# A one-core Hymba encoder layer: the PSUM banks of the keys' projection and of the first scores, and the planning weight of the last two residual chains

## The chip, the cores and the metric

The kernel runs on one core of a Trainium2 chip, as one program. The metric is the device time of one execution in microseconds (us). A few runs give a median; one more execution was recorded by the hardware profiler, and every row below comes from that one. PE is the matrix engine (TensorE), DVE the vector engine, ACT the scalar engine, POOL the GpSimd engine, and SP the queue that issues the DMA transfers. PSUM, into which PE writes its results, has eight banks of 128 x 512 float32 numbers.

## What is computed

```
mod = silu(c) @ w_ada + b_ada            # six vectors: sh1, sc1, gt1, sh2, sc2, gt2
h   = rmsnorm(x, g_pre_mix) * (1 + sc1) + sh1
proj = h @ w_in                          # q, k, v (512 columns each), then the Hyena group's 1536
q = rope(q); k = rope(k)
attn = dilated_window_attention(q, k, v) # 8 heads of 64
hy   = hyena_mixer(...)                  # long convolutions
mixed = concat(rmsnorm(attn, g_attn_out), rmsnorm(hy, g_hyena_out))
x = x + gt1 * rmsnorm(mixed @ w_out, g_post_mix)
h = rmsnorm(x, g_pre_mlp) * (1 + sc2) + sh2
x = x + gt2 * rmsnorm(square(relu(h @ w_mlp1)) @ w_mlp2, g_post_mlp)
```

One sequence of 512 tokens, width 1024, hidden width 4096, all float32.

## The kernel before

Every product is made from three matmuls: each operand is split into a high part and the rest (whi and wlo of a weight, hh and hl of the activations), and high times high, high times rest and rest times high are summed in one bank (`mm3`, line 605). A weight block of 128 x 512 is loaded by one DMA into a tile `raw`; ACT makes whi, and DVE or POOL makes wlo = raw - whi (`wload`, line 617).

The program is not issued in the order in which it is written. Every operation is recorded, and `Plan.order()` (line 290) then sets the order of each engine's instructions by simulating them with estimated durations. Where several operations are ready it takes the one with the largest priority: the length of the chain that hangs on it, plus a bias, plus a weight `urgent` that the code sets by `plan.local`. Operations with a weight of 600 or more may also be taken if they can start up to 0.5 us after the earliest ready one, those of 1000 or more up to 1.4 us, all others 0.02 us (line 379). An engine issues its instructions strictly in that order, so one that waits holds up everything behind it.

PSUM's eight banks are divided by tags: four of tag pj, two of ps, two of pi. A tile gets a bank of its tag when the previous tile in that bank has been read for the last time. `PS4(n, ..)` (line 593) gives four banks: the four pj for even n, and ps, ps, pi, pi for odd n.

The parts that the rows below speak of:

- The queries (banks pj552 to pj555), keys (pj598 to pj601) and values (pj644 to pj647) are projected one after the other by `proj_tok`, each into the four pj banks. `rotary` (line 1141) reads the queries' and keys' banks on DVE: for each token tile one product ra over 512 columns, two rb of 256, and a sum ra + rb on DVE or POOL.
- Beside them run the Hyena group's inverse transforms, whose results (inv487, inv522, inv523) stand in pi banks until DVE has read them into y512, y545 and y548.
- Also beside them run the late column sums of w_ada (`ada_acc`, line 831): eight blocks `raw` one after another, each added to `acc` by one DVE instruction, with three buffers (tag ra) for accumulator and blocks together; PE then makes a column of `acc` in a pj bank (pa, line 874). acc589 is the sum over raw590 to raw597, acc635 that over raw636 to raw643.
- Attention goes over four pairs of heads. For each pair the queries and keys are turned (pqk704 and pqk707 for the first pair, in ps banks); then for each of four query blocks the scores of two heads are made (s741 and s742 first), masked on DVE, put through exp on ACT, turned (ptr745, ..) and multiplied with the values (pav735, ..). Output projection of the Hyena group (pw) fills PE between them (`out_bank`, line 1216).
- After attention, for each token tile tt, `residual(tt)` (line 1315) is a chain on DVE and ACT: y times gate G, a norm factor ry, the new residual xr, a second norm factor r2, and dg, a diagonal matrix of r2. tt 0 has dg1009, tt 1 dg1016, tt 2 dg1031 and tt 3 dg1038. `to_h2` (line 1326) multiplies xr with dg on PE into ph banks: ph1017 to ph1023 for tiles 0 and 1, ph1039 to ph1045 for tiles 2 and 3. The first block of the MLP (pm) runs over the first 256 tokens and then over the second 256.

Of the kernel before, what the change touches and what calls it, by code (L numbers as in the profile page):

```python
# [554 lines left out]
def tile_hymba_layer(ctx, tc, t, out):  # L555
    nc = tc.nc
    plan = Plan(nc)
# [23 lines left out]
    def S(tag, s="u", dt=F32):  # L581
        return plan.tile(HOME.get(tag, "up"), tag, NB[tag], [P, 512], dt, s)
# [7 lines left out]
    def PS(s="ps", tag="ps"):  # L590
        return plan.tile("pp", tag, 4 if tag == "pj" else 2, [P, 512], F32, s)

    def PS4(n, s):

        return [PS(s, tg) for tg in (("pj",) * 4, ("ps", "ps", "pi", "pi"))[n % 2]]

    def T1(s="t", tag="t1"):
        return plan.tile("tiny", tag, 16, [P, 8], F32, s)
# [6 lines left out]
    def mm3(ps, lh, ll, rh, rl, start, stop):  # L605
        pe.matmul(ps, lh, rh, start=start, stop=False)
        pe.matmul(ps, lh, rl, start=False, stop=False)
        pe.matmul(ps, ll, rh, start=False, stop=stop)
# [8 lines left out]
    def wload(src):  # L617
        raw = S("raw", "raw")
        pre_loads.append(sp.dma_start(raw, src))
        hi, lo = wpair()  # L620
        act.copy(hi, raw)
        lo_of(vp, lo, raw, hi)
        return hi, lo
# [58 lines left out]
    ps = PS("pf", "pi")  # L682
# [4 lines left out]
    ps = PS("pf", "pi")  # L687
# [207 lines left out]
    def step(gen, n=1):  # L895
        for _ in range(n):
            next(gen, None)
# [38 lines left out]
    for d in range(8):  # L936
        ps = PS("px", "pj")
# [9 lines left out]
    for c in range(4):  # L947
        plan.bias = 2900.0 - 100.0 * c
        s = slice(2 * c, 2 * c + 2)
# [47 lines left out]
                mm3(banks[i], wh[:, s], wl[:, s], hT[k][0], hT[k][1], k == 0, k == 7)  # L997
        return banks

    def proj_tok(c0):  # L1000

        banks = [PS("pj", "pj") for _ in range(4)]
        for k in range(8):
            wh, wl = wload(w_in[k * P:(k + 1) * P, c0:c0 + 512])
            for i in range(4):
                s = slice(i * P, (i + 1) * P)
                mm3(banks[i], hT[k][0][:, s], hT[k][1][:, s], wh, wl, k == 0, k == 7)
        return banks
# [132 lines left out]
    def rotary(banks):  # L1141
        res = []
        for tt in range(4):
            a, b = S("qk", "ra"), S("cv", "rb")
            ps4 = banks[tt].rearrange("p (h d) -> p h d", h=NH)
            c_ = rope[:, tt, 0][:, None, :].to_broadcast([P, NH, 64])
            dve.tensor_tensor(out=a.rearrange("p (h d) -> p h d", h=NH), in0=ps4, in1=c_, op=ALU.mult)
            psw = banks[tt].rearrange("p (h s d) -> p h s d", h=NH, s=2)
            bw = b.rearrange("p (h s d) -> p h s d", h=NH, s=2)
            for s_ in range(2):  # L1150
                sn = rope[:, tt, 1, s_ * 32:s_ * 32 + 32][:, None, :].to_broadcast([P, NH, 32])
                dve.tensor_tensor(out=bw[:, :, s_, :], in0=psw[:, :, 1 - s_, :], in1=sn, op=ALU.mult)
            vp.tensor_tensor(out=a, in0=a, in1=b, op=ALU.add)
            res.append(a)
        return res

    qr = rotary(proj_tok(0))
    step(late, 2)
    kr = rotary(proj_tok(512))
    step(late, 2)  # L1160
    vb = proj_tok(1024)
    step(late, 2)
    vh = {}
# [48 lines left out]
    def load_out(g, hf):  # L1212
        row0 = W if g == 0 else 0
        return [wload(w_out[row0 + k * P:row0 + (k + 1) * P, hf * 512:hf * 512 + 512]) for k in range(4)]

    def out_bank(g, tt, hf, m_, ws, tag):

        s = slice(tt * P, (tt + 1) * P)
        bank = PS("pw", tag)
        for k in range(4):  # L1220
            mm3(bank, m_[k][0][:, s], m_[k][1][:, s], ws[k][0], ws[k][1], k == 0, k == 3)
        evac(g, tt, hf, bank)
# [10 lines left out]
    def heads(hp2):  # L1233


        tr = []
        for src, scl in ((qr, -0.125), (kr, 1.0)):
            ps = PS("pqk")
            pe.turn(ps, [src[tt][:, hp2 * P:(hp2 + 1) * P] for tt in range(4)], ident)
            hi, lo = R("cv", "qh"), R("cv", "ql")  # L1240
            act.activation(hi, ps, AF.Copy, scale=scl)
            dve.scalar_tensor_tensor(out=lo, in0=ps, scalar=scl, in1=f(hi), op0=ALU.mult, op1=ALU.subtract)
            tr.append((hi, lo))
        return tr

    qk = [heads(0)]
    for hp2 in range(4):
        (qh, ql), (kh, kl) = qk[hp2]
        a = S("vx", "att")
        att.append(a)  # L1250
        if hp2 == 1:
            step(late, 1)
        if hp2 == 0:
            wg0 = [load_out(0, hf) for hf in range(2)]
        rows = slice(0, 64), slice(64, 128)
        po = [PS("pav", "pi") for _ in range(2)]
        for qb in range(4):
            qs = slice(qb * P, (qb + 1) * P)
            o = slice((qb % 2) * P, (qb % 2 + 1) * P)
            if qb % 2 == 0:  # L1260
                pts = [(plan.tile("att", "pt", NPT, [P, 4, 256], F32R, "pth"),
                        plan.tile("att", "pt", NPT, [P, 4, 256], F32R, "ptl")) for _ in range(2)]

            pss = [PS("s", "pj") for _ in range(2)]
            pe.pair(pss, [[(x[r, qs], y[r, :]) for x, y in ((qh, kh), (qh, kl), (ql, kh))] for r in rows])
            for hh in range(2):
                h, ps = hp2 * 2 + hh, pss[hh]
                pth, ptl = pts[hh]
                sc = S("cv", "sc")
                st = T1("st", "st")  # L1270
                dve.tensor_tensor_reduce(out=sc, in0=ps, in1=mask[:, 384 - qb * P:896 - qb * P], scale=1.0,
                                         scalar=3e38, op0=ALU.add, op1=ALU.min, accum_out=st[:, 0:1])
                last_exp = [act.activation(sc, sc, AF.Exp, bias=st[:, 0:1], scale=-1.0, accum_out=st[:, 2:3])]
                dve.reciprocal(st[:, 3:4], st[:, 2:3])
                if qb == 3 or h < 3 and qb == 1:
                    act.activation(sc, sc, AF.Copy, scale=st[:, 3:4])
                else:
                    pool.tensor_tensor(out=sc, in0=sc, in1=st[:, 3:4].to_broadcast([P, 512]), op=ALU.mult)
                pt = PS("ptr")
                pe.turn(pt, [sc[:, kt * P:(kt + 1) * P] for kt in range(4)], ident)  # L1280
                p3 = pt.rearrange("p (k q) -> p k q", k=4)
                act.copy(pth[:, :, o], p3)
                dve.tensor_tensor(out=ptl[:, :, o], in0=p3, in1=f(pth[:, :, o]), op=ALU.subtract)
                if qb % 2:
                    o2 = slice((qb - 1) * P, (qb + 1) * P)
                    for kt in range(4):
                        vv = vh[kt, h // 4][:, (h % 4) * P:(h % 4 + 1) * P]
                        pe.matmul(po[hh][:, o2], vv, pth[:, kt], start=kt == 0, stop=False)
                        pe.matmul(po[hh][:, o2], vv, ptl[:, kt], start=False, stop=kt == 3)
            if qb == 1 and hp2 < 3:  # L1290
                qk.append(heads(hp2 + 1))

            for u in FILL.get((hp2, qb), ()):
                out_bank(0, u % 4, u // 4, mh, wg0[u // 4], "pj")
        for hh in range(2):
            r = rows[hh]
            act.copy(a[r, :], po[hh][64:128, :])
            dve.tensor_tensor(out=a[r, :], in0=po[hh][0:64, :], in1=a[r, :], op=ALU.add)
# [50 lines left out]
    for tt in range(4):  # L1349
        plan.bias = 200.0 * (4 - tt)  # L1350
        for hf in range(2):
            out_bank(1, tt, hf, ma, wo[hf], "pj" if tt < 2 else ("ps", "pi")[hf])
        plan.local = 700.0 * (tt < 2)
        dgs.append(residual(tt))
        plan.local = 0.0
        if tt % 2:
            plan.bias = 400.0
            plan.local = 700.0 if tt == 1 else 0.0
            to_h2(tt // 2, dgs[-2:])
            plan.local = 0.0  # L1360
# [15 lines left out]
    for half in range(2):  # L1376
        hid = []
        for cc in range(4):
            c0 = half * 2048 + cc * 512
            banks = PS4(cc + 1, "pm")  # L1380
            ws = [wload(w_1[k * P:(k + 1) * P, c0:c0 + 512]) for k in range(8)]
            for th in range(2) if half == 0 and cc == 0 else (None,):
                ts = slice(0, 512) if th is None else slice(th * 256, th * 256 + 256)
                for k in range(8):
                    for i in range(4):
                        s = slice(i * P, (i + 1) * P)
# [10 lines left out]
        for hf in range(2):  # L1397
            cs = slice(hf * 512, hf * 512 + 512)
            banks = PS4(hf + 1, "pf")
            nk = 8 if (half, hf) == (1, 1) else 16  # L1400
            for k in range(nk):
                r0 = half * 2048 + k * P
                wh, wl = wload(w_2[r0:r0 + P, cs])
                for tt in range(4):
                    s = slice(tt * P, (tt + 1) * P)
# [3 lines left out]
            for tt in range(4):  # L1409
                s = slice(tt * P, (tt + 1) * P)  # L1410
# [65 lines left out]
```

## Time and profile before

| | |
|---|---|
| median of 3 runs | 756.44 us (755.32 to 757.17) |
| the profiled execution | 760.61 us; span from first to last instruction 758.8 us |
| mean granted clock of PE, as a share of full speed | 0.986 |
| PE busy | 726.2 us, 96% of the span |
| DVE, ACT, POOL busy | 462.1, 325.1 and 80.9 us |

The granted clock has two levels here, 1.00 (2.4 GHz) and 0.50 (1.2 GHz). A number in brackets at the end of a timeline's row is the idle time of the engine just before it, and the arrow names what ended that time. Durations overlap: a matmul's row begins before the one ahead of it has ended, so rates are read from the starts. A wait for several semaphores is put down to the one that came last.

### The profile page before, as it was taken

Reading aid. Unit: us, or ns where it says so; the run is one execution under the profiler, and the core shown is the slowest. Engines: PE = TensorE matmul, PEld = TensorE weight load, DVE = VectorE, ACT = ScalarE, POOL = GpSimd, SP = SyncE. Lnnn points to the kernel's source line nnn. Section 1 sums busy time; section 2 is a strip of 40 time slices with the busy share of each in tenths; the row PEclk is TensorE's granted clock in tenths of the full one; section 3 lists DMA queues with packets and bytes.
Section 4 is the critical chain, followed back from the end, with each engine's and each line's share of the span. In section 5 each row is a group of like instructions: output and inputs, shape, how many; then the busy total and the mean of one; then the engine's idle time right before and its main releaser. Section 6 shows DMA issues by size and latency. Waiting matters only on the chain.

```text
span 758.8 us, 10203 instructions
## 1 busy us (share of the span) xinstructions
PE 726.2 (96%) x3648; PEld 587.7 (77%) x3648; DVE 462.1 (61%) x886; ACT 325.1 (43%) x631; POOL 80.9 (11%) x80
## 2 busy tenths in 40 slices
PE   5999999999999798999979999999999999999995
PEld 2667878988887676878879888888888888888874
DVE  5597974989686688997786844223222554232256
ACT  5545542234224267898575443213322353232132
POOL 0110400113030012343211000000000000000000
PEclk9999999999999899999989999999999999999998
DMA  9995244423615264261022533222223242123212
GB/s 291 359 391 183 84 153 152 126 98 120 209 34 153 73 217 155 84 192 59 29 93 79 187 106 118 84 84 70 97 81 100 84 152 98 56 75 111 98 50 111
DMA packets 55602, 96.68 MB, mean 127 GB/s; under 512 B 5853, under 2 KB 14301, under 8 KB 55296
## 3 DMA queue, kind: packets, MB, share of 16 engines
q1 hardware_dynamic: 54400, 91.58, 36.7%
q0 software_dynamic: 1008, 4.40, 1.6%
q8 instruction: 28, 0.46, 0.3%
q14 instruction: 22, 0.18, 0.1%
q10 hardware_dynamic: 144, 0.06, 0.0%
HBM read 91.56 MB, written 4.46 MB: 127 GB/s over the span
## 4 chain that ended last, share of the span: by engine, by line
PE 84%; DVE 6%; DMA 5%; ACT 3%; issue 1%; SPq 1%; POOL 0%; DVEq 0%; ACTq 0%; POOLq 0%
PE pm L513 24%; PE pf L513 21%; PE pj L513 17%; PE pw L513 4%; PE pH L513 3%; PE inv L513 3%; DMA raw<-in_w_ada_dram 2%; PE pe L513 2%; DMA raw<-in_w_in_dram 2%; PE pav L513 2%; PE ptr L461 1%; PE po L513 1%; PE s L473 1%; PE ph L513 1%; PE pa L513 1%
## 5 line engine op out<-in xcount | busy, mean ns | idle before, releaser
L513 DVE TENSOR_TENSOR wlo<-raw,whi 128x512 fp32r<-128x512 f32 x177 | 121.1, 696 | 164.7 <-ACT whi L513 94.7
L513 ACT CAST whi<-raw 128x512 fp32r<-128x512 f32 x192 | 116.8, 620 | 192.2 <-PE pf L513 92.0
L513 PE MATMUL pm<-h2l,whi 128*128 128x512 f32 (+1 forms) x288 | 88.3, 370 | 0.3 <-POOL h2l L513 0.3
L513 PE MATMUL pm<-h2h,whi 128*128 128x512 f32 (+1 forms) x288 | 88.2, 371 | 0.2 <-ACT h2h L513 0.2
L513 PE MATMUL pm<-h2h,wlo 128*128 128x512 f32 (+1 forms) x288 | 87.8, 370 | 0.0
L513 PE MATMUL pf<-whi,gl 128*128 128x512 f32 x256 | 85.5, 390 | 0.0
L513 PE MATMUL pf<-wlo,gh 128*128 128x512 f32 x256 | 84.7, 390 | 0.0
L513 PE MATMUL pf<-whi,gh 128*128 128x512 f32 x256 | 84.3, 392 | 0.1
L513 PEld LDWEIGHTS pm<-h2h,whi 128*128 128x128 f32 x288 | 51.7, 188 | 11.0 <-ACT h2h L513 1.0
L513 PEld LDWEIGHTS pm<-h2l,whi 128*128 128x128 f32 x288 | 51.9, 188 | 10.5 <-POOL h2l L513 0.5
L513 PEld LDWEIGHTS pm<-h2h,wlo 128*128 128x128 f32 x288 | 51.7, 188 | 10.3 <-DVE wlo L513 0.5
L513 PEld LDWEIGHTS pf<-whi,gh 128*128 128x128 f32 x256 | 47.8, 188 | 11.6 <-ACT whi L513 0.8
L513 PEld LDWEIGHTS pf<-whi,gl 128*128 128x128 f32 x256 | 48.1, 188 | 10.3
L513 PEld LDWEIGHTS pf<-wlo,gh 128*128 128x128 f32 x256 | 47.6, 188 | 10.8
L513 DVE SCALAR_TENSOR_TENSOR acc<-raw,vec,acc 128x512 f32<-128x512 f32 x56 | 42.7, 763 | 17.3 <-DMA raw<-in_w_ada_dram 17.0
L513 DVE TENSOR_TENSOR r<-r 128x512 f32<-128x512 f32 x32 | 21.7, 687 | 43.2 <-ACT r L513 43.2
L513 ACT ACTIVATE r<-pm 128x512 f32<-128x512 f32 x32 | 18.6, 596 | 53.3 <-PE pm L513 53.3
L513 PE MATMUL pj<-hh,whi 128*128 128x512 f32 x96 | 35.2, 397 | 0.8 <-ACT hh L513 0.8
L513 PE MATMUL pj<-hl,whi 128*128 128x512 f32 x96 | 36.0, 401 | 0.0
L513 POOL TENSOR_TENSOR wlo<-raw,whi 128x512 fp32r<-128x512 f32 x15 | 20.7, 1393 | 142.7 <-PE pj L513 37.8
L513 PE MATMUL pj<-whi,hh 128*128 128x512 f32 x96 | 35.6, 410 | 0.0
L513 PE MATMUL pj<-hh,wlo 128*128 128x512 f32 x96 | 35.4, 397 | 0.0
(245 smaller groups left out, 1360.6 us busy)
## 6 DMA issues: line engine op xcount, KB each, us to landing
raw<-in_w_mlp_dram SPq DMA_DIRECT2D x128, 256.0 KB, 2.8
raw<-in_w_ada_dram SPq DMA_DIRECT2D x96, 256.0 KB, 3.2
raw<-in_w_in_dram SPq DMA_DIRECT2D x48, 256.0 KB, 3.3
raw<-in_w_out_dram SPq DMA_DIRECT2D x16, 256.0 KB, 3.0
H<-hd SPq DMA_DIRECT2D x9, 256.0 KB, 4.9
x<-in_x_dram SPq DMA_DIRECT2D x8, 256.0 KB, 4.7
hd<-H SPq DMA_DIRECT2D x8, 256.0 KB, 2.0
xr<-in_x_dram SPq DMA_DIRECT2D x8, 256.0 KB, 5.1
```

Of the source, the lines that this page charges most:

```text
L461: plan.nc.tensor.transpose(out.ap()[:, i * P:(i + 1) * P], v.ap(), ident.ap())
L473: plan.nc.tensor.matmul(out.ap(), ts[i][0].ap(), ts[i][1].ap(), start=i == 0, stop=i == n - 1)
L513: getattr(e, meth)(*[real(a) for a in args], **{k: real(a) for k, a in kw.items()})
```

## The change

The keys' projection no longer goes into the four pj banks but into ps, ps, pi, pi. The first scores of the first pair of heads go into pi banks (query block 0) and ps banks (query block 1) instead of pj. The residual chains of token tiles 2 and 3 get the weight 650 in place of none.

```diff
-    def proj_tok(c0):
-
-        banks = [PS("pj", "pj") for _ in range(4)]
+    def proj_tok(c0, n=0):
+
+        banks = PS4(n, "pj")
...
     qr = rotary(proj_tok(0))
     step(late, 2)
-    kr = rotary(proj_tok(512))
+    kr = rotary(proj_tok(512, 1))
     step(late, 2)
     vb = proj_tok(1024)
...
-            pss = [PS("s", "pj") for _ in range(2)]
+
+            pss = [PS("s", "pj" if hp2 or qb > 1 else ("pi", "ps")[qb]) for _ in range(2)]
...
-        plan.local = 700.0 * (tt < 2)
+        plan.local = 700.0 * (tt < 2) + 650.0 * (tt > 1)
         dgs.append(residual(tt))
```

PE, ACT and SP issue the same instructions as before, and on balance two of DVE's go to POOL. What changes is the order. In the rows below the number behind the underscore differs between the kernels and means nothing; the name ahead of it is the same tile in both.

**PE, the end of the keys' projection (pj599 to pj601) and the start of the values' (pj644, pj645).** Before:

```order
L513 MATMUL pj601_2475<-wlo625_2527,hh146_725 128x512
L513 MATMUL inv523_2424<-ib211_403,yl543_2394 128x258
L513 MATMUL pj601_2475<-whi624_2519,hl147_735 128x512
L513 MATMUL pa634_2631<-ones2_79,acc589_2192 128x1 x2
L513 MATMUL pj644_2636<-whi649_2533,hh87_336 128x512
L513 MATMUL pj645_2638<-whi649_2533,hh87_336 128x512
L513 MATMUL pj644_2636<-wlo650_2542,hh87_336 128x512
```

With the change:

```order
L513 MATMUL pj601_2493<-whi624_2530,hh146_725 128x512
L513 MATMUL pj644_2619<-whi649_2547,hh87_336 128x512
L513 MATMUL pj601_2493<-wlo625_2544,hh146_725 128x512
L513 MATMUL pj644_2619<-wlo650_2557,hh87_336 128x512
L513 MATMUL pj601_2493<-whi624_2530,hl147_735 128x512
L513 MATMUL pj644_2619<-whi649_2547,hl88_348 128x512
L513 MATMUL pj645_2630<-whi649_2547,hh87_336 128x512
```

The column sum pa634, which waited for a pj bank, no longer stands between the two, and the values' matmuls are mixed with the keys' last ones. 22 values' matmuls then follow the keys' last one before the first transposes pqk704, and 6 more before pqk707; before, pqk704 stood ahead of 57 of the keys' 96 matmuls. Farther on, s741 stands ahead of 60 of the values' 96 matmuls and ptr745 ahead of 7; before, s741 came directly behind the last of them.

**DVE, the reads of the inverse transforms.** Before:

```order
L513 SCALAR_TENSOR_TENSOR acc589_2192<-raw592_2252,vec7_71,acc589_2192 128x512
L513 SCALAR_TENSOR_TENSOR acc589_2192<-raw593_2409,vec7_71,acc589_2192 128x512
L513 TENSOR_TENSOR y545_2457<-inv522_2293,q544_2450 128x255 x2
L513 COPY y545_2457<-inv522_2293 128x2
L513 TENSOR_TENSOR sc2214_2469<-pa588_2342,vec7_71 128x4
L513 TENSOR_TENSOR hyo546_2472<-y545_2457,hy464_1901 128x512
```

With the change:

```order
L513 SCALAR_TENSOR_TENSOR acc589_2192<-raw593_2388,vec7_71,acc589_2192 128x512
L513 SCALAR_TENSOR_TENSOR acc589_2192<-raw594_2394,vec7_71,acc589_2192 128x512
L513 TENSOR_TENSOR y545_2449<-inv522_2293,q544_2435 128x255 x2
L513 COPY y545_2449<-inv522_2293 128x2
L513 TENSOR_TENSOR hyo546_2467<-y545_2449,hy464_1901 128x512
L513 SCALAR_TENSOR_TENSOR acc589_2192<-raw595_2442,vec7_71,acc589_2192 128x512
L513 TENSOR_TENSOR y548_2481<-inv523_2407,q547_2474 128x255 x2
L513 COPY y548_2481<-inv523_2407 128x2
```

y548, the read of inv523, stood inside the keys' rotary (some 30 instructions later) and now stands well ahead of it; but the steps of acc589 for the blocks raw594 and raw595 moved ahead of y545 and y548.

**DVE, from the second tile's xr957 to its dg1016.** Before:

```order
L513 SCALAR_TENSOR_TENSOR xr957_3630<-y778_3097,ry1013_4121,xr957_3630 128x512
L513 SCALAR_TENSOR_TENSOR xr958_3637<-y885_3644,ry1013_4121,xr958_3637 128x512
L513 SCALAR_TENSOR_TENSOR y832_3504<-pw1032_3980,gr954_4009,y832_3504 128x512
L513 TENSOR_TENSOR r21015_4153<-s21014_4140 128x1
L513 TENSOR_TENSOR wlo1076_4155<-raw1074_3953,whi1075_4112 128x512
L513 SCALAR_TENSOR_TENSOR y932_4099<-pw1033_4094,gr954_4009,y932_4099 128x512
L513 RECIPROCAL r21015_4153<-r21015_4153 128x1
L513 TENSOR_SCALAR dg1016_4169<-ident1_81,r21015_4153 128x128
```

With the change:

```order
L513 SCALAR_TENSOR_TENSOR xr957_3595<-y778_3110,ry1013_4108,xr957_3595 128x512
L513 SCALAR_TENSOR_TENSOR xr958_3602<-y885_3669,ry1013_4108,xr958_3602 128x512
L513 TENSOR_TENSOR wlo1070_4130<-raw1068_3891,whi1069_4103 128x512
L513 TENSOR_TENSOR wlo1073_4136<-raw1071_3936,whi1072_3973 128x512
L513 TENSOR_TENSOR r21015_4145<-s21014_4127 128x1
L513 TENSOR_TENSOR wlo1076_4147<-raw1074_3948,whi1075_4120 128x512
L513 RECIPROCAL r21015_4145<-r21015_4145 128x1
L513 TENSOR_SCALAR dg1016_4157<-ident1_81,r21015_4145 128x128
```

The reads of banks pw1032 and pw1033 (y832, y932) moved behind dg1016, and two wlo, which POOL made before, came in. POOL, which made four wlo between dg1009 and dg1016 or just ahead (wlo1067, wlo1073, wlo1070, wlo1079), has two of them left, and ACT makes the cast for the second, wlo1079, later than before. Farther on, the chains of tiles 2 and 3 end together: dg1031 and dg1038 are two instructions apart, where eight lay between them.

## Rows read from the trace of the kernel before

**Rows 1.** The page's part 1: each engine's busy us, share of the span and instructions.
```profile
PE 726.2 (96%) x3648; PEld 587.7 (77%) x3648; DVE 462.1 (61%) x886; ACT 325.1 (43%) x631; POOL 80.9 (11%) x80
```

**Rows 2.** Waits of PE: us in total, times, longest.
```profile
PE pa L513 <- DVE rb L513: 5.8, 1, 5.8
PE ph L513 <- DVE dg L513: 4.1, 1, 4.1
```

**Rows 3.** Busy time, PEclk and DMA in five stretches.
```profile
251.40:257.00 5.60, 5.60 (x16) 4.47 (x17) 4.90 (x12) 1.24 (x2) 0.40 (x1) 0.58 0.17 47
293.60:297.00 3.40, 3.40 (x18) 3.29 (x17) 2.47 (x5) 2.80 (x6) 0.00 (x0) 0.50 0.53 153
297.00:365.00 68.00, 67.75 (x441) 54.51 (x439) 58.31 (x137) 56.73 (x118) 22.19 (x19) 1.00 0.32 101
382.40:389.10 6.70, 4.74 (x22) 4.74 (x23) 5.38 (x14) 4.29 (x12) 1.33 (x1) 0.50 0.29 101
410.00:744.00 334.00, 333.90 (x1480) 272.06 (x1479) 130.41 (x204) 110.84 (x196) 0.00 (x0) 1.00 0.29 97
```

**Rows 4.** Timeline of PE: start, us, instruction [idle before <-releaser].
```profile
250.59 0.99 PE L513 MATMUL pa<-ones,acc 128*128 128x1 f32 x4 [5.80 <-DVE rb L513]
251.44 1.20 PE L513 MATMUL pj<-whi,hh 128*128 128x512 f32 x2
...
255.00 1.05 PE L513 MATMUL pj<-wlo,hh 128*128 128x512 f32 x2
...
256.41 0.62 PE L513 MATMUL pj<-whi,hh 128*128 128x512 f32 x2
256.87 0.64 PE L513 MATMUL pj<-wlo,hh 128*128 128x512 f32 x2
```

**Rows 5.** Timeline of DVE, 222 to 254 us.
```profile
226.64 0.75 DVE L513 SCALAR_TENSOR_TENSOR acc<-raw,vec,acc 128x512 f32<-128x512 f32 x1 [2.69 <-DMA raw<-in_w_ada_dram]
...
244.62 1.77 DVE L513 TENSOR_TENSOR wlo<-raw,whi 128x512 fp32r<-128x512 f32 x1
246.32 0.41 DVE L513 TENSOR_TENSOR rb<-pj,rope 128x256 f32<-128x256 f32 x1
...
251.69 1.88 DVE L513 TENSOR_TENSOR ra<-ra,rb 128x512 f32<-128x512 f32 x3
```

**Rows 6.** Timeline of PE where attention starts.
```profile
279.66 0.80 PE L513 MATMUL pa<-ones,acc 128*128 128x1 f32 x6 [0.66 <-DVE acc L513]
...
291.76 0.66 PE L461 MATMUL ptr<-ident,sc 128*128 128x128 f32 x4 [1.26 <-DVE ptl L513]
293.09 0.39 PE L513 MATMUL pav<-pth,vh 128*128 128x256 f32 x1 [0.68 <-ACT pth L513]
```

**Rows 7.** Timeline of DVE before and at the second dg.
```profile
375.39 1.79 DVE L513 TENSOR_TENSOR y<-y,G 128x512 f32<-128x512 f32 x1
377.11 1.23 DVE L513 TENSOR_TENSOR ry<-sy 128x1 f32<-128x1 f32 x1
378.26 0.68 DVE L513 TENSOR_TENSOR y<-y,G 128x512 f32<-128x512 f32 x1
...
379.05 2.44 DVE L513 SCALAR_TENSOR_TENSOR xr<-y,ry,xr 128x512 f32<-128x512 f32 x2
...
383.86 0.44 DVE L513 TENSOR_SCALAR dg<-ident,r 128x128 f32<-128x128 f32 x1
```

**Rows 8.** Timeline of POOL in the same stretch.
```profile
374.09 4.23 POOL L513 TENSOR_TENSOR wlo<-raw,whi 128x512 fp32r<-128x512 f32 x3 [24.92 <-ACT r L513]
379.26 1.68 POOL L513 TENSOR_TENSOR wlo<-raw,whi 128x512 fp32r<-128x512 f32 x1 [0.94 <-ACT whi L513]
```

**Rows 9.** Timeline of PE around the first half of the MLP's first block.
```profile
384.36 5.23 PE L513 MATMUL ph<-dg,xr 128*128 128x128 f32 x24 [4.06 <-DVE dg L513]
...
401.71 2.92 PE L513 MATMUL ph<-dg,xr 128*128 128x128 f32 x24
...
406.46 0.51 PE L513 MATMUL pm<-h2l,whi 128*128 128x256 f32 x2 [0.31 <-POOL h2l L513]
```

## The prediction

> **What bounds the kernel now.** I read the page's first part first: PE is busy for 96% of the span [rows 1], so a change can win only what PE loses, and no other engine's busy time matters by itself. The list of PE's waits comes next. Two are long, 5.8 us for the keys' rotary and 4.1 us for a dg [rows 2]. Then I asked which stretches have a clock below full speed or PE not filling the time. Attention from 297 us (67.75 of 68.00 us) and the MLP (333.90 of 334.00) have neither [rows 3]: what is won ahead of them should reach the end undiminished. Three places do have such losses, and the change touches all three.
>
> Place 1, the end of the keys' projection. PE stands for 5.80 us until rb instructions have emptied a pj bank, and after it runs at clock 0.50 until about 256 us: five pairs of matmuls, from 251.44 to 255.00, take 1.05 to 1.20 us where a pair takes 0.62 or 0.64 afterwards [rows 3, 4]. With the part of a sixth that is about 5 x 0.43 = 2.2 us more. DVE shows why the rotary is late: the wlo ahead of it took 1.77 us, until 246.39, and the rotary then lasts from 246.32 to 253.57 [rows 5].
>
> Place 2, the start of attention. PE waits 0.66, 1.26 and 0.68 us, and the clock is 0.50 from 293.60 to 297.00, which costs half of 3.40, 1.70 us [rows 3, 6]. Together 4.3 us.
>
> Place 3, the residual. PE waits 4.06 us for dg1016, after which 24 ph matmuls take 5.23 us at clock 0.50 where the same 24 later take 2.92 [rows 3, 9]: 2.2 to 2.3 us more. Smaller waits come to 0.15 + 0.31 us at 405.65 and 406.46; the row with the second is shown [rows 9]. DVE is slow there in three instructions: y times G 1.79 us, ry (one column) 1.23 us, and one of the two xr that share 2.44 us, while POOL runs wlo [rows 7, 8]. Undisturbed, the other y times G takes 0.68 us, and one column next to nothing, so about 1.1 us are lost in each, 3.3 us in all.
>
> **The change part by part.** The work is the same, so everything is a matter of order.
>
> *Keys in the other banks.* The values' projection needs the pj banks, which the queries have left long before, so the wait of 5.80 us and the 2.2 us of clock behind it go: 8.0 us. The rotary now lies beside the values' matmuls and ends in front of pqk707. What covers it: 28 matmuls at 0.23 us (two in 0.46 us, from 256.41 to 256.87 [rows 4]), 6.5 us, and about 0.5 us of transposes. What it takes: 253.57 - 246.32 less one foreign y of 0.33, 6.9 us [rows 5], and a handover of some 0.2 to 0.4 us. I take a rest of 0.4 us that PE waits. Its ends are 0, and 1.6 if DVE begins as late behind the keys' last matmul as it does now (246.32 against an end at 244.8).
>
> The price is in the banks that the keys now take. Two of them hold inv487 and inv523 or inv522 until DVE has read them, and in DVE's order steps of acc589 now stand ahead of those reads. A step that has to await its block is costly: DVE stood 2.69 us for the DMA and then took 0.75 [rows 5], so 3.4 us a block, with few buffers to load ahead. But at 226.64 the chain held a buffer that the column sum before it still occupied. That sum's matmuls (pa588) come earlier in the new order, so two blocks can be under way. I take 0.7 us, nearer to "landed in time"; the ends are 0 and one whole block, 3.4. Place 1 then gives 8.0 - 0.4 - 0.7 = 6.9 us.
>
> *First scores in pi and ps.* They no longer queue behind the values in the pj banks. In the new order s741 stands ahead of 60 of the values' matmuls where it stood behind all, so the chain of mask, exp and cast up to ptr745 has up to 53 matmuls, 12 us, of cover. What stays is ACT's and DVE's chain itself between the transposes: I keep the waits of 1.26 and 0.68, for ptl and pth [rows 6], and let the 0.66 and the 1.70 of clock go: 2.4 us. Ends: 0 (all of it comes back) and 4.3.
>
> *Weight 650 for tiles 2 and 3.* Oddly it helps tile 1. Between xr957 and dg1016 two bank reads leave and two wlo come in, all of 128 x 512, which I take as even. But POOL has two wlo left where four slowed three of DVE's instructions. The first of them ended before y times G began (374.09 plus a third of 4.23, [rows 7, 8]). If the second comes too late to slow anything 3.3 us go, if it slows one 2.2; I take 3.0. dg1016 ends near 381.3 instead of 384.3. PE has two matmuls fewer ahead of it (0.46 us), so it still waits about 1.5 us instead of 4.06. Whether the clock falls there no row tells: after the 0.66 us it did not, after the 1.26 and 0.68 it did [rows 3, 6]. I side with the first. So the MLP's first half starts 3.0 + 2.2 = 5.2 us earlier. It then ends 5.2 us earlier too, near 395.7, where ph of tiles 2 and 3 begins (401.71 less 0.8 for eight of its matmuls that stood ahead, less 5.2 [rows 9]). dg1031 and dg1038 now stand together, at about 397: DVE's order ends both chains together, and dg1038 has eight instructions fewer between it and dg1031. That leaves a new wait of 1.5 us, and takes the small ones of 0.46 away, of which I count 0.4. Place 3: 5.2 - 1.5 + 0.4 = 4.1 us. Ends: 0, if dg1038 comes no earlier than now, and 5.6.
>
> **Sum.** 6.9 + 2.4 + 4.1 = 13.4 us. The profiled execution would go from 760.61 to 747.2. It lay 4.17 us above the median of the runs, 756.44, so the median goes to 743.0. No stage behind the places can eat this by waiting for data: in the MLP DVE is busy for 130.41 of 334 us and the DMA engines for a share of 0.29 [rows 3].
>
> **The rivals.** A run-to-run spread of 755.32 to 757.17 means that about 0.3%, 2.3 us, can be told from nothing.
>
> *(a) Part is given back.* Any of three mechanisms does it. The clock falls at the two waits that I leave (1.7 at attention, 2.2 at place 3): gain 13.4 - 3.9 = 9.5. The pi banks await one w_ada block in full (3.4 instead of 0.7): 10.7. Or place 3 only moves its wait to ph1039, because dg1038 is no earlier: 13.4 - 4.1 = 9.3. For it: all three waits hang on DVE, which is near full there (4.90 of 5.60 us, 5.38 of 6.70 [rows 3]). One of them leaves 745.7 to 747.1, two together 749.6 to 751.0. I give the clock 0.12, the banks 0.10 and dg1038 0.08.
>
> The Trainium skill has a rule for the first of these. "TensorE: Matmul & The Clock Gate", section "A second HAM failure mode: psum-queue depth-cycling", says that a PE which idles only briefly but often between groups of matmuls, as it goes round its banks, can lose its clock as it does after one long stop. By this rule the clock falls at both places and the time is 756.44 - 9.5 = 746.9; by the row after the 0.66 us it falls at neither. The trace agrees with the rule only in part: a fall follows the 1.26 and 0.68 and none follows the 0.66.
>
> *(b) The wait only changes its name: same time.* If the 5.80 us at place 1 are DVE's whole load and not a bank, PE runs into the same lateness at pqk707 or at the values' later weights (wlo662 stands behind the rotary). Against it: DVE was idle for 2.69 us at 226.64 and the wait ends with an rb, not with a sum [rows 4, 5]. It would keep 8.0 of the 13.4 away, and with the ends 0 of place 2 and 1.5 lost at place 3 it gives a gain of about 1.5: 755.
>
> *(c) Slower: the w_ada chain becomes PE's path.* Five steps of acc589 (raw593 to raw597) and one of acc635 stand ahead of the keys' rotary, three of them ahead of the reads that free the keys' banks. If each awaits its own block at 3.4 us, six cost 20.6 us, of which 0.7 is counted already: 756.44 - 13.4 + 19.9 = 762.9. From four uncovered blocks on (13.7 us) the gain is gone. Against it: only three stand in front of the bank reads, the others run beside the keys' last matmuls, and two buffers overlap a load with a step.
>
> **How the numbers follow.** The likeliest, all three places about as summed, gets 0.58, with a range of its own from 739.5 (the good ends of all three places are 13.4 + 1.1 + 1.9 + 1.5 = 17.9, of which I grant 16.9) to 745.5. Case (a) gets 0.30, 745.5 to 751, of which 0.03 lies beyond 750.5. Case (b) gets 0.06, and (c) 0.06, half of which still ends under 759. Faster by over 0.3%: 0.58 + 0.30 = 0.88; same 0.06; slower 0.06. A range from 739.5 to 750.5 leaves out (b), (c), and a tail of (a) and of the likeliest, about 0.18.
>
> **What the changed profile would show.** Right: no wait of PE for rb, the clock at 1.00 from the keys to the transposes, the first pav at about 283.8 instead of 293.1, a wait for dg1016 under 2 us followed by full clock, and one for dg1031 or dg1038 of 1 to 2 us at ph. Wrong: PE waits for y545, y548 or y512 in front of pj600 (bank); for ql or ra at pqk707 (rotary); 24 ph at 5.2 us (clock); a wait of 4 us or more at ph1039; or gaps inside attention, which had none.

## The result, and the profile with the change

| | before | with the change |
|---|---|---|
| median | 756.81 us (4 runs, 755.32 to 757.56) | 750.97 us (4 runs, 750.51 to 752.28) |
| the profiled execution | 760.61 us, span 758.8 | 750.51 us, span 748.7 |
| mean granted clock in it | 0.986 | 0.995 |

The ratio is 0.9928, with a 95% interval of 0.9908 to 0.9948: faster by 5.8 us, where 13.4 were forecast, and 0.5 us outside the range. The profiled span fell by 10.1 us. So there are two gaps to explain: from 13.4 to 10.1 within the profile, and from 10.1 to 5.8 between the profile and the medians. The 5.8 rests on four runs of each kernel; a later session (experiment 2) measured 8.3 us between the same two kernels.

The list of PE's waits with the change (us in total, times, longest), which answers to [rows 2]:

```profile
PE pm L513 <- DVE y L513: 2.1, 1, 2.1
PE pw L513 <- DVE st L513: 1.2, 1, 1.2
...
PE pj L513 <- DVE y L513: 0.4, 1, 0.4
...
PE ph L513 <- DVE dg L513: 0.3, 1, 0.3
```

The wait for rb (5.8) is gone and the one for dg (4.1) has shrunk to 0.3. In their place stand 2.1 us of pm for a y, which no part of the prediction names, and 1.2 us of pw for st, at 279.61. The pi banks, which I had priced at 0.7 us, cost 0.4 (pj for y).

Four stretches (columns as in [rows 3], the granted clock third from the end):

```profile
244.00:258.00 14.00, 14.00 (x76) 11.42 (x75) 10.13 (x24) 3.37 (x5) 2.55 (x2) 1.00 0.26 74
380.50:383.00 2.50, 0.39 (x4) 0.27 (x3) 2.50 (x3) 1.45 (x5) 0.96 (x1) 1.00 0.18 55
383.10:386.40 3.30, 3.30 (x18) 3.30 (x17) 2.92 (x6) 2.94 (x8) 1.48 (x2) 0.50 0.08 28
405.00:735.00 330.00, 329.92 (x1443) 267.97 (x1442) 128.70 (x202) 108.78 (x193) 0.00 (x0) 1.00 0.30 96
```

The clock is 1.00 through the handover from keys to values, where it was 0.58; the MLP is as full as before. The only stretch at 0.50 between the start and the end lies behind the wait of pm: PE works for 0.39 of 2.50 us, and the clock then is 0.50 for 3.4 us, which costs 1.7.

PE where the keys hand over, and the first pav:

```profile
250.63 0.60 PE L461 MATMUL pqk<-ident,ra 128*128 128x128 f32 x4
...
253.04 0.63 PE L461 MATMUL pqk<-ident,ra 128*128 128x128 f32 x4
...
256.10 0.50 PE L473 MATMUL s<-qh,qh 64*128 64x512 f32 x2
...
284.98 0.86 PE L513 MATMUL pav<-pth,vh 128*128 128x256 f32 x2 [0.36 <-ACT pth L513]
```

pqk704, pqk707 and s741 come without a wait; s741 starts at 256.10 where it started at 277.82, and the first pav at 284.98 where [rows 6] has 293.09. So the lead there is 8.1 us. It is 8.7 at the first matmul of tile 1's output projection (367.19 before, 358.53 now) and 10.0 at the last of the MLP's first block (417.49, 407.54). Places 1 and 2 together gave 8.7 of the 9.3 us that I had summed; place 3 gave 1.3 of 4.1.

Place 3: DVE, then PE, then POOL.

```profile
366.52 0.97 DVE L513 TENSOR_TENSOR y<-y,G 128x512 f32<-128x512 f32 x1
367.42 0.15 DVE L513 TENSOR_TENSOR ry<-sy 128x1 f32<-128x1 f32 x1
...
368.27 1.42 DVE L513 SCALAR_TENSOR_TENSOR xr<-y,ry,xr 128x512 f32<-128x512 f32 x2
...
371.77 0.28 DVE L513 TENSOR_SCALAR dg<-ident,r 128x128 f32<-128x128 f32 x1
...
379.58 2.43 DVE L513 SCALAR_TENSOR_TENSOR xr<-y,ry,xr 128x512 f32<-128x512 f32 x2
381.93 1.40 DVE L513 SCALAR_TENSOR_TENSOR y<-pw,gr,y 128x512 f32<-128x512 f32 x2
```

```profile
372.11 2.94 PE L513 MATMUL ph<-dg,xr 128*128 128x128 f32 x24 [0.34 <-DVE dg L513]
...
380.34 0.28 PE L513 MATMUL pm<-h2l,whi 128*128 128x256 f32 x1
382.73 0.39 PE L513 MATMUL pm<-h2h,whi 128*128 128x256 f32 x1 [2.11 <-DVE y L513]
```

```profile
379.79 1.67 POOL L513 TENSOR_TENSOR wlo<-raw,whi 128x512 fp32r<-128x512 f32 x1 [5.33 <-ACT whi L513]
```

Compare with [rows 7]: y times G takes 0.97 instead of 1.79 us, ry 0.15 instead of 1.23, the two xr 1.42 instead of 2.44, nearly as forecast. Of POOL's two wlo that are left, one runs from 365.66 to 366.94 and still delays y times G (0.68 undisturbed); beside ry and the two xr POOL does not work. dg1016 is ready when PE is. But y832 and y932, the reads of the output banks pw1032 and pw1033, start at 381.93, behind tile 2's two xr, which share 2.43 us because POOL's wlo lies beside them. The banks are the ps and pi banks in which the MLP's first block is to accumulate. PE does the matmuls for which it has banks, stops at 380.62 and goes on at 382.73, when the first read has ended.

### The profile page after: what moved, and what is told of

It is laid out like the page before. It is cut to its first block, busy times and chain, and to the rows that moved or that the text cites. A ratio compares the mean times of both kernels' runs of the same rounds, so it can differ in the third digit from the quotient of the medians.

```text
span 748.7 us, 10200 instructions
## 1 busy us (share of the span) xinstructions
PE 722.3 (96%) x3648; PEld 583.7 (78%) x3648; DVE 463.9 (62%) x884; ACT 325.1 (43%) x631; POOL 83.7 (11%) x82
## 4 chain that ended last, share of the span: by engine, by line
PE 83%; DVE 9%; DMA 4%; ACT 2%; issue 1%; SPq 0%; POOL 0%; DVEq 0%; ACTq 0%
PE pm L513 24%; PE pf L513 22%; PE pj L513 16%; PE pw L513 4%; PE pH L513 3%; PE pav L513 2%; PE inv L513 2%; PE ptr L461 2%; PE s L473 2%; PE pe L513 2%; DMA raw<-in_w_ada_dram 2%; PE po L513 1%; DMA raw<-in_w_out_dram 1%; DVE y L513 1%; DMA x<-in_x_dram 1%
## 5 line engine op out<-in xcount | busy, mean ns | idle before, releaser
L513 PE MATMUL pm<-h2h,whi 128*128 128x512 f32 (+1 forms) x288 | 90.9, 373 | 2.2 <-DVE y L513 2.1
L513 PE MATMUL pm<-h2l,whi 128*128 128x512 f32 (+1 forms) x288 | 90.7, 372 | 0.3 <-POOL h2l L513 0.3
L513 PE MATMUL pm<-h2h,wlo 128*128 128x512 f32 (+1 forms) x288 | 90.4, 373 | 0.0
L513 PEld LDWEIGHTS pm<-h2h,whi 128*128 128x128 f32 x288 | 53.4, 191 | 12.9 <-DVE y L513 2.3
L513 PEld LDWEIGHTS pm<-h2l,whi 128*128 128x128 f32 x288 | 53.5, 191 | 10.5 <-POOL h2l L513 0.5
L513 PEld LDWEIGHTS pf<-whi,gl 128*128 128x128 f32 x256 | 48.1, 188 | 10.2
L513 DVE SCALAR_TENSOR_TENSOR acc<-raw,vec,acc 128x512 f32<-128x512 f32 x56 | 44.6, 796 | 10.2 <-DMA raw<-in_w_ada_dram 9.9
L513 PE MATMUL pj<-wlo,hh 128*128 128x512 f32 x96 | 34.9, 399 | 0.0
```

The costliest lines, as they stand in the source:

```text
L513: getattr(e, meth)(*[real(a) for a in args], **{k: real(a) for k, a in kw.items()})
```

## Experiments

Times are compared with runs of the kernel before on the same chip in the same session.

**1. The kernel before, unchanged.** Is its profile a typical execution?

> The kernel before, unchanged, once more. Its profiled execution was 760.61 us, some 4 us above the median of its runs, while that of the changed kernel lay with its runs. Theory 1: these 4 us are stretches at clock 0.50 (after its three waits) that are not the same in every execution; then this profile has a span between 752 and 757 us, the same waits of about 5.8, 4.1 and 1.3 us, and fewer or shorter stretches at 0.50. Theory 2: being profiled costs this kernel 4 us; then the span is 758 to 759 again while the timed runs stay near 756.8. The ratio is 1.000 within 0.3% by both.

757.63 us (12 runs) against 757.67 (23 runs), ratio 1.0001 (0.9985 to 1.0017); span 754.8, clock 0.993. PE's two long waits, and three stretches:

```profile
PE pa L513 <- DVE rb L513: 4.4, 1, 4.4
...
PE ph L513 <- DVE dg L513: 4.1, 1, 4.1
```

```profile
248.90:252.20 3.30, 3.30 (x11) 2.72 (x11) 3.30 (x9) 0.00 (x0) 1.00 (x1) 0.50 0.00 0
293.60:297.00 3.40, 3.38 (x23) 2.65 (x23) 3.17 (x5) 1.50 (x3) 0.00 (x0) 1.00 0.40 118
382.00:385.40 3.40, 3.40 (x19) 3.40 (x18) 2.73 (x7) 2.33 (x6) 0.00 (x0) 0.50 0.30 89
```

The wait for dg is the same as in [rows 2], but the one for rb is 1.4 us shorter, and the clock is 0.50 for 3.4 us at place 1, not at all at place 2 (it is 1.00 from 252.3 to 382.0, where [rows 3] have 0.50 from 293.6 to 297.0), and for 3.4 us at place 3. In the profile on which the prediction rests it was 0.50 for 6.8, 3.4 and 6.8 us. That is 10.2 us less at half speed, but PE stood idle in part of them. Followed matmul by matmul, the second execution is 0.5 us ahead where place 1 begins, gains 1.4 by the shorter wait, 0.9 by the clock behind it, 0.2 at place 2, 0.7 by the clock at place 3 and 0.3 later: 4.0 us, of which the clock is not quite half. At place 2 the matmuls that had run at 0.50 took only 0.6 us less at full clock, not 1.7, as a wait of 0.31 us for pth came out.

The wait for rb is shorter because of the wlo ahead of the rotary, 1.77 us in [rows 5]. Here it takes 0.68, since DVE begins it before POOL begins a wlo of its own; in the first profile POOL was 0.04 us ahead. POOL before, then DVE and POOL here:

```profile
244.58 1.26 POOL L513 TENSOR_TENSOR wlo<-raw,whi 128x512 fp32r<-128x512 f32 x1 [24.71 <-PE inv L513]
```

```profile
243.81 0.68 DVE L513 TENSOR_TENSOR wlo<-raw,whi 128x512 fp32r<-128x512 f32 x1
```

```profile
244.06 1.56 POOL L513 TENSOR_TENSOR wlo<-raw,whi 128x512 fp32r<-128x512 f32 x1 [24.73 <-PE inv L513]
```

That is 1.1 of the 1.4 us; the other 0.3 are a w_ada block that landed earlier. The weight alone and the scores alone (experiment 2), with the keys in the pj banks too, wait 4.4 and 4.2 us for rb: 5.8 was the exception.

In 63 executions of this kernel in three sessions the mean clock ran from 0.980 to 0.993 (median 0.988) and the time from 754.72 to 763.01 us (median 758.28), shorter where the clock was higher. The first profile's clock of 0.986 or a lower one is in 19 of the 63; the second's 0.993 is the highest there is, in 3. So theory 2 fails, and theory 1 holds in part: the stretches at 0.50 differ from execution to execution, but they are less than half of the difference here, and the wait for rb, which it took to be fixed, is not. The first profile lies 2.3 us above the median of the 63, and the three runs with a median of 756.44 lay 1.8 below it.

**2. Each part by itself, and two together.** The edits are the diff's three parts: `proj_tok(512, 1)`, `("pi", "ps")[qb]`, and `+ 650.0 * (tt > 1)`.

Keys alone:

> The keys' projection in the other banks alone. Theory A: place 1 is worth 7 us (no wait for rb, no stretch at 0.50 after it, little wait at the pi banks), and the first scores' waits of 0.7, 1.3 and 0.7 us with their stretch at 0.50 stay: ratio 0.990 to 0.994 if the runs lose at place 1 what the profile shows, span 751.5 to 752.5. Theory B: the runs lose less there than the profile, by the clock: ratio 0.994 to 0.997. Theory C: the scores' banks bring nothing of their own, and this kernel is as fast as keys and scores together.

754.42 us, ratio 0.9952 (0.9937 to 0.9966). The wait for rb is gone. The ratio is in the range of theory B, but the clock at place 1 is not all of it: the first scores still need pj banks, so s741 starts at 270.65, and the start of attention loses more than before, 3.4 us in waits and two stretches at clock 0.50:

```profile
274.20:277.50 3.30, 3.30 (x11) 1.81 (x10) 2.56 (x9) 2.12 (x4) 0.73 (x1) 0.50 0.88 307
287.90:294.60 6.70, 6.46 (x29) 5.72 (x28) 5.09 (x8) 3.73 (x7) 0.00 (x0) 0.50 0.48 150
```

Scores alone:

> The first scores in pi and ps banks alone, the keys' projection in the pj banks as before. If the two parts act together: place 1 keeps its wait for rb of 4 to 6 us, and the scores, which come behind the keys' rotary, cannot start much earlier, ratio 0.997 to 1.001. If the scores' banks bring the 6 us by which keys and scores together beat the keys alone, 0.991 to 0.994.

759.88 us, ratio 1.0016 (1.0000 to 1.0031): nothing, or a little slower, close to what the first theory said. But its reason was wrong in part: s741 does start early, at 260.27 instead of 277.82, and yet the first pav comes at 292.69, only 0.4 us earlier. The two long waits remain:

```profile
PE ph L513 <- DVE dg L513: 4.5, 1, 4.5
PE pa L513 <- DVE rb L513: 4.2, 1, 4.2
```

Weight alone:

> The weight for tiles 2 and 3 alone. Theory A (bank reads come late): the wait for dg of 4.1 us is gone or under 1.5, a wait of pm for y of about 2 us stands in its place, and the span falls by 1 to 2.5 us, ratio 0.997 to 0.999. Theory B (the prediction's sum): it falls by 4 us, ratio about 0.995, with a wait at ph for dg of tiles 2 and 3.

757.91 us, ratio 0.9999 (0.9980 to 1.0018). Neither theory: the wait for dg stays and no wait of pm for y appears, as y832 and y932 still stand ahead of dg1016 in its order.

```profile
PE ph L513 <- DVE dg L513: 3.9, 1, 3.9
```

Keys and scores, without the weight:

> The changed kernel without the weight for tiles 2 and 3. Theory A: the weight gave little, since it moved the reads of banks pw1032 and pw1033 (y832, y932) behind two residual vectors and the MLP's first block then waits 2.1 us for those banks and loses the clock: then this kernel keeps 8.5 us of the 10.1 by which the profiled span fell, 750 to 751 us, with the wait for dg of about 4 us back and no wait of pm for y; ratio 0.993 to 0.996. Theory B, the prediction's: the weight is worth 4 us: span 752.5 to 753, ratio 0.997 to 1.000.

748.50 us, ratio 0.9877 (0.9861 to 0.9894); and again, beside other kernels:

> Keys and scores in the other banks without the weight, once more, beside the versions below. If the weight costs about 2 us on top of them: 748 to 749 us, ratio 0.986 to 0.989, waits for dg of 1.7 and 0.7 us, and no stretch at clock 0.50 between the start and the end.

748.46 us, ratio 0.9869 (0.9856 to 0.9882). This is faster than the changed kernel, by more than theory A allowed. The waits of its first profile, and DVE at place 3:

```profile
PE ph L513 <- DVE dg L513: 2.3, 2, 1.7
...
PE pw L513 <- DVE st L513: 1.1, 1, 1.1
```

```profile
370.64 0.75 DVE L513 SCALAR_TENSOR_TENSOR y<-pw,gr,y 128x512 f32<-128x512 f32 x1
...
371.50 0.46 DVE L513 TENSOR_SCALAR dg<-ident,r 128x128 f32<-128x128 f32 x1
...
379.36 0.73 DVE L513 SCALAR_TENSOR_TENSOR y<-pw,gr,y 128x512 f32<-128x512 f32 x1
380.01 2.19 DVE L513 SCALAR_TENSOR_TENSOR xr<-y,ry,xr 128x512 f32<-128x512 f32 x2
```

The wait for dg did not come back as 4 us: it is 0.7 us for dg1016 and 1.7 for dg1038. y832 is read ahead of dg1016 here and y932 ahead of tile 2's xr, so pm waits for no y. In the first of the two profiles the clock is 1.00 from 14.7 us until PE has finished; in the second there is one stretch at 0.50, behind a wait of 1.56 us of pw for st.

The changed kernel once more, in a session with the scores alone and the first kernels of 3 and 4:

> The changed kernel once more, beside the kernels that it is compared with. Theory A: the weight costs time on top of the two changes of banks; its ratio is again 0.991 to 0.995, above the 0.9877 of the kernel without the weight, with the wait of pm for y of about 2 us and a stretch at clock 0.50 behind it. Rival: the difference of 0.5% was one of sessions, and the ratio is 0.987 to 0.989.

750.22 us against 758.50, ratio 0.9892 (0.9872 to 0.9912), again with 2.1 us of pm for y and the clock at 0.50 behind it. The ratio misses both ranges: it lies below theory A's and just above the rival's, so part of the 0.5% was one of sessions. Nine runs of the changed kernel have a median of 750.65, nine of keys and scores 748.47; no session had both, and the intervals of their ratios overlap. The traces agree with a cost: tile 1's output projection begins at 357.76 here and at 357.69 in the first profile of keys and scores, the last matmul of the MLP's first block at 406.65 and 405.10. So the weight costs about 2 us on top of the other two parts, 1.6 of them at place 3.

Which part made dg1016 early? From the first matmul of tile 1's output projection (pw1010) to the start of dg1016 it takes:

| kernel | us |
|---|---|
| before, two profiles | 16.67, 16.68 |
| weight alone | 16.67 |
| keys and scores | 13.81 |
| with the change | 13.24 |
| before, POOL without these wlo (below) | 12.91 |

So of the 3.4 us by which dg1016 is earlier, which I had credited to the weight (as 3.0), 2.9 come with the two changes of banks: in their order wlo1070 and wlo1073 are DVE's already, and POOL keeps wlo1067 and wlo1079, as in the changed kernel.

**3. Does POOL slow DVE at place 3?**

```diff
-            ws = [wload(w_1[k * P:(k + 1) * P, c0:c0 + 512]) for k in range(8)]
+            ws = [wload(w_1[k * P:(k + 1) * P, c0:c0 + 512], dve if c0 == 0 else None) for k in range(8)]
```

(`wload` makes wlo on the engine given, else on DVE or POOL as before.)

> The kernel before, with the wlo of the MLP's first eight blocks made by DVE alone and none by POOL. The prediction took 1.1 us off each of three DVE instructions that ran beside these wlo on POOL. If that is so, y times G takes 0.7 us here, ry under 0.2 and the two xr 1.4 together, dg1016 stands 3 us or more earlier against the start of xr955, and PE waits for it under 1.5 us instead of 4.1; the wlo that now come later may be waited for by pm instead. If the slowness has another cause, these instructions keep 1.8, 1.2 and 2.4 us.

One run: 757.08 us. DVE, and PE's waits:

```profile
373.76 0.68 DVE L513 TENSOR_TENSOR y<-y,G 128x512 f32<-128x512 f32 x1
374.70 0.16 DVE L513 TENSOR_TENSOR ry<-sy 128x1 f32<-128x1 f32 x1 [0.25 <-ACT junk L513]
...
375.57 1.42 DVE L513 SCALAR_TENSOR_TENSOR xr<-y,ry,xr 128x512 f32<-128x512 f32 x2
...
379.10 0.28 DVE L513 TENSOR_SCALAR dg<-ident,r 128x128 f32<-128x128 f32 x1
```

```profile
PE pm L513 <- DVE y L513: 1.4, 1, 1.4
PE ph L513 <- DVE dg L513: 1.2, 2, 0.8
```

0.68, 0.16 and 1.42 us: all three are fast, and dg1016 comes 3.8 us earlier. PE waits 1.2 us for dg in two pieces, but now 1.4 for y932, which stands far back in DVE's order. The price of 1.1 us an instruction was right.

**4. Can the bank reads be put back?** The changed kernel with

```diff
-... op0=ALU.mult, op1=ALU.add)
+... op0=ALU.mult, op1=ALU.add, urgent=640.0 * (tt > 2))
```

in the read of a bank of the output projection (`evac`, line 1210).

> The changed kernel with the reads of banks pw1032 and pw1033 (y832, y932) at a weight of 640, so that they stand ahead of dg1016 again; the residual chains keep their 650. Theory A: pm no longer waits for y and the clock does not fall there, dg1016 comes 0.7 us later; 3 us less than the changed kernel, ratio 0.987 to 0.990. Rival (the loss lies with the later chains, dg1031 and dg1038 or the mixing of both): the ratio stays at 0.992 to 0.994 though the wait of pm for y is gone, with a longer wait at ph for dg1031 or dg1038.

749.97 us, ratio 0.9887 (0.9866 to 0.9909): in theory A's range, but the same as the changed kernel beside it (0.9892), and not 3 us less. The wait of pm for y is gone, which shows that it was the place of these reads. But the planner now gives wlo1076 and a y times G to POOL:

```profile
371.10 2.39 DVE L513 TENSOR_TENSOR wlo<-raw,whi 128x512 fp32r<-128x512 f32 x2
...
374.87 1.07 DVE L513 TENSOR_SCALAR dg<-ident,r 128x128 f32<-128x128 f32 x1
```

```profile
370.55 1.79 POOL L513 TENSOR_TENSOR wlo<-raw,whi 128x512 fp32r<-128x512 f32 x1 [2.10 <-DVE xr L513]
374.58 1.27 POOL L513 TENSOR_TENSOR y<-y,G 128x512 f32<-128x512 f32 x1 [2.24 <-ACT junk L513]
```

```profile
PE ph L513 <- DVE dg L513: 2.3, 1, 2.3
```

Two wlo of DVE take 2.39 us instead of 1.29 and dg1016 itself 1.07 instead of 0.28, and PE waits 2.3 us for it, with a stretch at 0.50 from 375.8 to 379.1. The loss went to another name.

Then the changed kernel with the edit of 3:

> The changed kernel with the wlo of the MLP's first eight blocks made by DVE alone. y832 and y932 stand behind dg1016 and the reads of ph, as in the changed kernel, but ahead by the POOL instruction that slowed xr959 and xr960 (2.4 us for two). If the wait of pm for y comes from the place of the bank reads alone it stays at 2 us; if POOL's share in their lateness counts it falls to 1 us or less. In time 748 to 751 us.

755.95 us, ratio 0.9955 (0.9937 to 0.9972): slower than the changed kernel by more than 5 us, outside what was expected. PE's waits:

```profile
PE pm L513 <- DVE y L513: 4.0, 1, 4.0
...
PE pm L513 <- ACT whi L513: 1.8, 2, 1.0
```

y832 starts at 381.11, 9.1 us behind dg1016 where it stood 10.2 behind it in the changed kernel, and yet the wait is twice as long. PE also waits for whi. The trace shows why: wlo1070, which DVE made at 369.60 in the changed kernel, comes at 386.14, and PE has 16 matmuls of pm ahead of the one that waits for the bank, where it had 40. It lacked the late wlo, and with them the work that had filled the time up to the bank's release. Two versions without the weight were to beat keys and scores: best_a has the edit of 3 and the bank reads at 1000, best_b the bank reads at 640.

> Keys and scores in the other banks, no weight for tiles 2 and 3, the wlo of the MLP's first block on DVE alone, and the reads of pw1032 and pw1033 at a weight of 1000: DVE has nothing that POOL slows, y832 stands just ahead of dg1016 and y932 right behind the first reads of ph. Expected: waits for dg under 0.7 us before the first half, none of pm for y, and 1 us or less before the second half; 746.5 to 748.5 us, ratio 0.984 to 0.988. If the later wlo are now too late for pm: no gain over keys and scores, 748 to 750.

> Keys and scores in the other banks with the bank reads at a weight of 640, POOL's part left as the planner has it. By the theory that POOL's instructions beside DVE make dg1016 late, the y times G that goes to POOL here slows dg as it did with the changed kernel's early reads: a wait for dg of about 2 us at the first half, ratio 0.987 to 0.990. If it does not slow it: 0.984 to 0.987.

749.78 (ratio 0.9881, 0.9868 to 0.9894) and 750.42 us (0.9889, 0.9876 to 0.9902): no better. best_a waits 0.3 us for dg1016 and pays the rest back with the late wlo, the second outcome named:

```profile
PE pm L513 <- DVE wlo L513: 2.3, 2, 2.1
...
PE ph L513 <- DVE dg L513: 0.3, 1, 0.3
```

best_b waits 0.9 us for dg1016 and 1.4 for dg1038, so the 2 us expected at the first half did not come: the y times G on POOL starts behind dg1016, which takes 0.29 us. It is POOL's wlo1076 that slows DVE there, one wlo of 1.79 us. Keys and scores alone stays the best version.

## Why the prediction was wrong, step by step

It forecast the direction and the main mechanism rightly, and a gain more than twice the measured one. Of the 7.6 us that are missing (13.4 - 5.8), 4.3 lie in the step from the profile to the median, 2.8 in place 3, and 0.6 in places 1 and 2 (0.1 goes the other way). The 4.3 are smaller in other runs: the later session has 8.3 us for the same change, and 63 executions of the kernel before against nine of the changed one 7.6 us (758.28 and 750.65).

*"It lay 4.17 us above the median of the runs, 756.44, so the median goes to 743.0."* This is the step that failed most. It takes for granted that the changed kernel's profiled execution would lie as far above its runs. It lay 0.5 us below them. The 4.17 us were no property of the kernel: 2.3 of them are the profile's distance from the median of the 63 executions, 1.8 the distance of three runs from it on the other side. My terms 5.80, 2.2, 1.7 and 2.2 us were all taken from that one execution. Another of the same kernel (experiment 1) has a wait of 4.4 us for rb, half of the stretch at clock 0.50 at place 1, none at place 2 and half at place 3. A loss that differs from run to run can be won back only to its mean.

*"Between xr957 and dg1016 two bank reads leave and two wlo come in, which I take as even."* Even for DVE, but I did not ask who waits for the banks that those reads free. It is the MLP's first block, whose tiles take ps, ps, pi and pi. The new wait of 2.1 us and the 1.7 us of clock behind it are most of the 4.06 and 2.2 that went. I looked for the next late thing at ph1039, where PE did not wait at all.

*"Weight 650 ... Oddly it helps tile 1."* A wrong attribution: I compared the order before with the order after all three edits and gave the change near dg1016 to the edit that stands next to it. The weight alone leaves that interval at 16.67 us, and the two banks alone shorten it to 13.81. The size, 3.0 against 3.4, was right for the wrong reason.

*Places 1 and 2*, 6.9 + 2.4 us, came out at 8.7 against the same trace, and at 5.6 against the second trace of the kernel before, where tile 1's output projection begins at 364.11. The rotary was covered entirely (0 for my 0.4) and the pi banks cost 0.4 for 0.7; rival (c) had no part, as the w_ada blocks were read in time. But the split between the two was wrong: neither edit brings its part alone (0.9952 and 1.0016), and together they bring more than the sum (0.9877). With the keys alone the start of attention loses clock while the scores wait for pj banks; with the scores alone the wait for rb stays, and an early s741 brings nothing by itself.

*Rival (a)* had the time, 749.6 to 751.0 for two of its mechanisms together, but by luck: none of the three came. In the profile the clock stayed at 1.00 behind the waits at the start of attention and behind dg1016, the pi banks cost 0.4 us, and PE did not wait at ph1039. The clock fell behind the wait of pm for y, which the rival does not name. The Trainium skill's section on psum-queue depth-cycling ("TensorE: Matmul & The Clock Gate") has short stops between groups of matmuls cost the clock. Here that is sometimes so: one execution of keys and scores had waits of 1.1, 0.7 and 1.7 us and no fall, another had a fall behind 1.56 us.

What is not settled: why best_b, with the clock at 0.995 to 0.998, is still 2 us slower than keys and scores (against the second profile of that kernel, with the same fall at 280 us and the same start of tile 1's output projection, 359.9, it is 1.1 us later at ph1039; the rest is open); why the scores alone win nothing though s741 is early; and whether another order has neither the wait for dg nor that for y. The versions tried moved the loss among the two and the weights.

## What to carry to other kernels

When an order moves a read of a PSUM bank, find the next tile in that bank and when PE wants it; an instruction that is late for DVE's own sake may be the one that PE waits for. Take clock losses and waits from several executions, not from the one in the trace, and forecast median against median; three runs gave 756.44 where 63 gave 758.28. With a list scheduler, attribute by orders of the single edits: an edit far ahead can make the change that stands beside another.

## What the runs showed of the hardware

The same program with the same waits lost clock in stretches of 3.4 or 6.8 us at a place, or not at all, from execution to execution. A wait of 4.06 us for dg1016 was followed by 6.8 us at 0.50 in one and by 3.4 in the other; 1.26 and 0.68 us at the start of attention by 3.4, and 1.35 and 0.67 by none. Over 63 executions the mean clock ran from 0.980 to 0.993 and the time over 8.3 us.

A DVE instruction with two operands and none of them in PSUM (wlo, y times G, xr, ry, dg), begun beside a running POOL instruction, lasts until that one has ended and then about its own time, however small it is: ry of one column took 1.23 us, dg 1.07, and without POOL 0.16 and 0.28. Which of the two begins first decides who waits (experiment 1: DVE 1.77 us behind POOL and 0.68 ahead of it, POOL 1.26 and 1.56). DVE instructions that read a PSUM bank, and reciprocals, were not slowed in the traces of the two kernels. An example is y932 with the reciprocal behind it in the kernel before, POOL and then DVE:

```profile
382.89 1.33 POOL L513 TENSOR_TENSOR wlo<-raw,whi 128x512 fp32r<-128x512 f32 x1 [1.95 <-ACT whi L513]
```

```profile
383.01 0.74 DVE L513 SCALAR_TENSOR_TENSOR y<-pw,gr,y 128x512 f32<-128x512 f32 x1
383.68 0.15 DVE L513 RECIPROCAL r<-r 128x1 f32<-128x1 f32 x1
```

The Trainium skill has this as an exclusive lock on a port pair shared by the two ("SBUF — State Buffer", section "Who interferes with whom"); the rows agree.
